# Two matmuls of 128 columns in place of a wide and a narrow one, in some tiles of a transposed product

## The chip, the cores and the metric

The kernel runs on one core of one Trainium2 chip. The metric is the device time of one execution in microseconds (us), as the median of several executions.

## What is computed

One layer of a decoder trunk on 256 tokens of width 2048, all in float32: an input projection, a Mamba-2 scan (SSD) beside sparse attention with a top-64 token indexer, one output projection, and an MLP with a squared ReLU four times as wide.

```python
def hybrid_layer(x, ...):
    h = rmsnorm(x, g_mix) @ w_in                  # 2048 -> 5728
    z, xbc, dt, q, k, v, qi, ki, wi = _split(h, IN_SIZES)
    xbc = jax.nn.silu(causal_dwconv(xbc, conv_w, conv_b))
    ...
    y_ssd = ...                                   # chunked scan, gated, normalised
    y_att = dsa_attention(q, k, v, qi, ki, wi)
    x = x + jnp.concatenate([y_ssd, y_att], axis=-1) @ w_out
    u = rmsnorm(x, g_mlp) @ w_up                  # 2048 -> 8192
    return x + jnp.square(jax.nn.relu(u)) @ w_down
```

## The kernel before

Every large product is made from split operands. `operands` (L113) loads a slab of weights (`raw`), casts it on ScalarE to the rounded float32r form `hi` (L125) and lets VectorE compute the rest `lo = raw - hi` (L126); the activations are kept as `hi` and `lo` too (`hx` for the input projection, `x2x` for the MLP). A product then needs three float32r matmuls for each pair of tiles: hi by hi, lo by hi and hi by lo.

There are two kinds of product. `product` (L138) puts tokens on partitions: the activations are the stationary operand, up to 512 weight columns move (lines L148 to L150). `product_t` (L184) puts columns on partitions: a 128x128 tile of weights is stationary, and the 256 tokens move. The row `right(kt)` holds, side by side, 256 columns of activations `hi` and 256 of `lo`. It runs over 4 slabs of 8 tiles, 32 tiles in all, into two accumulators of 512 columns in PSUM. The left half of an accumulator (columns 0 to T = 256) gathers hi by hi, the right half the two corrections; `total` (L207) adds the halves afterwards. `product_t` serves the index queries (`qi`, 4 products), the convolution's channels (`xbc`, 6 products) and the whole up-projection (`w_up`, 32 products). All its matmuls stand at L201.

TensorE's order is written by hand: the program order is the engine's order. Small matmuls of the scan, the indexer and the attention (transposes, scores, statistics) are tasks that `step()` lets in between tiles, at L204 after every fourth tile of `product_t`. Each takes a PSUM bank through `mp` (L131), which appends to the list `entry`; a finished `product` appends to it as well (L181). So `entry` is not empty exactly when other matmuls have run on TensorE since the last tile of a `product_t`.

Such a tile has a form of its own (L195 to L197). The ordinary tile is three matmuls of 256 columns: weights `hi` by x `hi`, weights `lo` by x `hi`, weights `hi` by x `lo`. Behind other matmuls it is two: weights `hi` by all 512 columns in one, then weights `lo` by x `hi`. Each matmul brings a load of its stationary tile of its own; the profile lists them under PEld.

In the MLP the order is: up-projection quarters 0 and 1 in one go, down-projection quarter 0, up 2, down 1, up 3, down 2, down 3 (L818 to L822). The first of the up-projection's products still has residual tasks between its tiles (`split_rows`, transposes at L672); after that nothing comes between the tiles until a `product` of the down-projection.

Of the kernel before, what the change touches and what calls it, by code (L numbers as in the profile page):

```python
# [16 lines left out]
P = 128  # L17
D = 2048
T = 256
# [49 lines left out]
def hymba_kernel(ctx: ExitStack, tc: tile.TileContext, xn, xt, w_in, w_out, w_up, w_down, vcol, vrow, out):  # L69
# [28 lines left out]
    def step():  # L98
        for t in list(tasks):
            if isinstance(t[1], int) and t[1] > 0:  # L100
                t[1] -= 1
            elif not isinstance(t[1], str) or t[1] in done:
                advance(t)
# [9 lines left out]
    def operands(src, n, load=None, shift=0):  # L113

        with tc.high_priority(offset=HP):
            raw = wts.tile([P, n], F32, name="raw", tag="raw", bufs=RB)
            both = wts.tile([P, 2 * n + SPARE], F32R, name="w2", tag="w2", bufs=WB)
            hi, lo = both[:, shift:shift + n], both[:, shift + n:shift + 2 * n]
            step = n if load is None else n // 2
            for i in range(0, n, step):  # L120
                s = slice(i, i + step)
                nc.sync.dma_start(raw[:, s], src[:, s])
                if load is not None:
                    load()
                nc.scalar.copy(hi[:, s], raw[:, s])  # L125
                nc.vector.tensor_tensor(lo[:, s], raw[:, s], hi[:, s].bitcast(F32), op=OP.subtract)  # L126
        return hi, lo

    entry = []

    def mp(name):  # L131
        entry.append(name)
        return ps.tile([P, 512], F32, name=name, tag="mid")

    def accumulators():
        return [ps.tile([P, 512], F32, name="acc", tag="acc") for _ in range(2)]

    def product(src, n, left, load=None, tail=None):  # L138


        acc = accumulators()
        last = KT if tail is None else KT - 4

        def part(kt, out, b, wh, wl):
            s = slice(b * P, (b + 1) * P)
            ah, al = left(kt)
            free = tail is not None
            nc.tensor.matmul(out, ah[:, s], wh, start=(kt == 0), stop=False, skip_group_check=free)  # L148
            nc.tensor.matmul(out, al[:, s], wh, start=False, stop=False, skip_group_check=free)  # L149
            nc.tensor.matmul(out, ah[:, s], wl, start=False, stop=(kt == KT - 1), skip_group_check=free)  # L150

        kept = []
        halves = [slice(0, n // 2), slice(n // 2, n)]
        if tail is not None:
            acc.append(mp("acc_t"))
        for kt in range(KT):
            if kt % 2 == 0:
                hi, lo = operands(src[kt // 2], 2 * n, load, 0 if tail is None else SPARE - SHIFT_T)
            w = slice(kt % 2 * n, kt % 2 * n + n)
            wh, wl = hi[:, w], lo[:, w]  # L160
            if tail is None:
                for b in range(NB):
                    part(kt, acc[b][:, :n], b, wh, wl)
            elif kt < last:
                for c in halves if kt else [slice(0, n)]:
                    part(kt, acc[0][:, c], 0, wh[:, c], wl[:, c])
                for i, c in enumerate(halves):
                    part(kt, acc[1 + i][:, c], 1, wh[:, c], wl[:, c])
            else:
                kept.append((kt, wh, wl))  # L170
            step()
        if tail is not None:
            for kt, wh, wl in kept:
                for c in halves:
                    part(kt, acc[0][:, c], 0, wh[:, c], wl[:, c])
            tail(0, slice(0, n), acc[0])
            for i, c in enumerate(halves):
                for kt, wh, wl in kept:
                    part(kt, acc[1 + i][:, c], 1, wh[:, c], wl[:, c])
                tail(1, c, acc[1 + i][:, c])  # L180
        entry.append("product")  # L181
        return acc

    def product_t(src, right):  # L184

        acc = accumulators()
        for i in range(4):
            hi, lo = operands(src[i], 1024, shift=SHIFT_T)
            c = i % 2
            for k in range(8):  # L190
                kt = 8 * (i // 2) + k
                x = right(kt)
                s = slice(k * P, (k + 1) * P)

                if entry:  # L195
                    entry.clear()
                    todo = [(hi, 0, 0, 2 * T), (lo, T, 0, T)]  # L197
                else:
                    todo = [(hi, 0, 0, T), (lo, T, 0, T), (hi, T, T, T)]
                for j, (w, at, fr, n) in enumerate(todo):  # L200
                    nc.tensor.matmul(acc[c][:, at:at + n], w[:, s], x[:, fr:fr + n], start=(kt + j == 0),  # L201
                                     stop=(kt == KT - 1 and j == len(todo) - 1), skip_group_check=True)
                if k % 4 == 3:
                    step()  # L204
        return acc
# [58 lines left out]
    def in_block(name, load=None):  # L264
        o, n = in_off[name]
        src = w_in[o:o + n * D].rearrange("(g p c) -> g p c", g=8, p=P)
        return product(src, n, h_left, load)

    def in_pair(name, i):
        o = in_off[name][0] + i * 256 * D  # L270
        return product_t(w_in[o:o + 256 * D].rearrange("(h p c) -> h p c", h=4, p=P), lambda kt: hx[:, kt, :])
# [39 lines left out]
    def stats():  # L311
        nc.sync.dma_start(vr, vrow)
        sst1 = small.tile([P, NB], F32, name="sst1", tag="sst1")
        nc.vector.tensor_reduce(out=sst1, in_=ss1, axis=AX.X, op=OP.add)
        rsqrt(rstd, sst1, 1.0 / D, "x", nc.vector)
        done.add("rstd")

        dg = mid.tile([P, NB, P], F32, name="dg", **u2)
        for b in range(NB):
            nc.vector.tensor_scalar(dg[:, b, :], ident, rstd[:, b:b + 1], None, op0=OP.mult)  # L320
        yield Y["rr"]
        pt = mp("ps_r")
        for b in range(NB):
            nc.tensor.matmul(pt[:, b * P:(b + 1) * P], ones, dg[:, b, :], start=True, stop=True)
        nc.scalar.copy(rrow, pt[:, :T])
# [9 lines left out]
    def transposes(src, n, name):  # L335
        pt = mp(f"pt_{name}")
        for i in range(n):
            nc.tensor.transpose(pt[:, i * P:(i + 1) * P], src[:, i * P:(i + 1) * P], ident)
        return pt
# [368 lines left out]
    def run():  # L708
# [58 lines left out]
        for j in range(4):  # L767
            spawn(residual(j, product(w_out[j], 512, y_left)), f"res{j}")
# [4 lines left out]
    def x2(kt):  # L773
        if kt >= KT - 4:
            need("res3")
        return box[0][:, kt, :]

    first = product_t(w_up[0], x2)
    while tasks:
        step()  # L780
# [11 lines left out]
    def up(q):  # L792
        uh = mlp.tile([P, KT, T], F32R, name="uh")
        ul = mlp.tile([P, KT, T], F32R, name="ul")
        for j in range(8):
            r = mlp.tile([P, 2, T], F32, name="r")
            total(r, first if q + j == 0 else product_t(w_up[8 * q + j], x2))
            nc.vector.scalar_tensor_tensor(r, r, 0.0, r, op0=OP.max, op1=OP.mult)
            s = slice(2 * j, 2 * j + 2)
            nc.scalar.copy(uh[:, s, :], r)  # L800
            nc.vector.tensor_tensor(ul[:, s, :], r, uh[:, s, :].bitcast(F32), op=OP.subtract)
        return uh, ul

    def down(q, u):
        for j in range(4):

            def add(b, c, acc):
                c = slice(512 * j + c.start, 512 * j + c.stop)
                nc.vector.scalar_tensor_tensor(xr[:, b, c], acc, rs4[:, b:b + 1], xr[:, b, c], op0=OP.mult, op1=OP.add)  # L809
                if q == 3:  # L810
                    nc.sync.dma_start(out[b * P:(b + 1) * P, c], xr[:, b, c])

            end = q == 3 and j == 3
            acc = product(w_down[4 * q + j], 512, lambda kt: (u[0][:, kt, :], u[1][:, kt, :]), tail=add if end else None)
            for b in range(0 if end else NB):
                add(b, slice(0, 512), acc[b])
# [58 lines left out]
```

## Time and profile before

| | us |
|---|---|
| median of 3 runs | 1104.3 (1104.14 to 1104.31) |
| the profiled execution's own time | 1106.19 |
| its span, first to last instruction | 1104.1 |
| TensorE busy with matmuls (PE), share of the span | 1093.8, 99% |
| TensorE weight loads (PEld) | 993.5, 90% |
| VectorE (DVE) | 691.8, 63% |
| ScalarE (ACT) | 534.3, 48% |
| 16 DMA engines, busy share of the main queue | 58.2% |

A matmul's listed duration runs from its start to the modelled end of its drain, and the next starts long before that, so what a matmul costs is read from start to start, or from the pieces of the chain of waits, which run from end to end: a piece with its time and its count gives the time for one.

### The profile page before, as it was taken

What the parts mean: (1) busy time and instruction counts of PE and PEld (TensorE: products, weight loads), DVE (VectorE), ACT (ScalarE), POOL (GpSimd) and SP (SyncE); (2) the same over time, 40 slices, a digit from 0 to 9 for tenths busy, and PEclk for the clock granted to TensorE, in tenths of its full rate; (3) what the DMA queues carried; (4) which work ended last, traced back from release to release, by engine and by line L of the source; (5) the groups of instructions that cost most, each with busy time, mean ns of one, the idle gap of its engine ahead of it and who ended that gap; (6) DMA issues with size and microseconds to landing.
All of it is one profiled execution on the core that took longest, in us unless ns stands there. A gap on an engine that the chain in (4) does not pass through costs nothing.

```text
span 1104.1 us, 17665 instructions
## 1 busy us (share of the span) xinstructions
PE 1093.8 (99%) x7052; PEld 993.5 (90%) x7052; DVE 691.8 (63%) x976; ACT 534.3 (48%) x749; POOL 42.5 (4%) x41
## 2 busy tenths in 40 slices
PE   9999998999999999999999999999999999999998
PEld 7999997888888899999998889998889999888888
DVE  6796989677765565666655545665555665555443
ACT  7755554555765544444444334444334454333331
POOL 0020131122000000000000000000000000000000
PEclk9999999999999999999999999999999999999999
DMA  9856444643375555555556655566665566666662
GB/s 296 277 204 189 147 119 151 213 155 120 128 248 189 175 189 186 184 187 191 189 182 194 199 191 191 191 194 193 197 196 193 192 192 193 196 195 197 209 210 77
DMA packets 63745, 207.53 MB, mean 188 GB/s; under 512 B 7216, under 2 KB 11568, under 8 KB 63664
## 3 DMA queue, kind: packets, MB, share of 16 engines
q1 hardware_dynamic: 63520, 206.36, 58.2%
q8 instruction: 55, 0.90, 0.3%
q14 instruction: 26, 0.21, 0.1%
q10 hardware_dynamic: 144, 0.05, 0.0%
HBM read 204.29 MB, written 2.10 MB: 187 GB/s over the span
## 4 chain that ended last, share of the span: by engine, by line
PE 92%; DVE 3%; DMA 3%; ACT 1%; issue 1%; SPq 0%; ACTq 0%; DVEq 0%
PE acc L201 40%; PE acc L150 16%; PE acc L148 16%; PE acc L149 16%; DMA raw<-in_w_in 2%; DVE bc L517 1%; DVE w L126 1%; PE ps_y L588 1%; DMA xrow<-in_xn 1%; DVE sc L481 1%; PE ps_sr L672 0%; PE ps_l L626 0%; PE ps_o L651 0%; ACT w L125 0%; PE ps_dec L579 0%
## 5 line engine op out<-in xcount | busy, mean ns | idle before, releaser
L126 DVE TENSOR_TENSOR w<-raw,w 128x1024 fp32r<-128x1024 f32 (+3 forms) x400 | 466.9, 1170 | 379.5 <-ACT w L125 378.8
L125 ACT CAST w<-raw 128x1024 fp32r<-128x1024 f32 (+3 forms) x400 | 399.5, 1002 | 492.6 <-PE acc L150 255.5
L201 PE MATMUL acc<-x2x,w 128*128 128x256 f32 (+1 forms) x3067 | 355.9, 279 | 0.0
L201 PEld LDWEIGHTS acc<-x2x,w 128*128 128x128 f32 x3067 | 355.3, 188 | 0.5
L148 PE MATMUL acc<-w,uh 128*128 128x512 f32 (+1 forms) x527 | 199.9, 379 | 0.0
L149 PE MATMUL acc<-w,ul 128*128 128x512 f32 (+1 forms) x527 | 199.8, 379 | 0.0
L150 PE MATMUL acc<-w,uh 128*128 128x512 f32 (+1 forms) x527 | 199.8, 379 | 0.0
L150 PEld LDWEIGHTS acc<-w,uh 128*128 128x128 f32 x527 | 98.9, 188 | 18.8
L148 PEld LDWEIGHTS acc<-w,uh 128*128 128x128 f32 x527 | 98.9, 188 | 18.7
L149 PEld LDWEIGHTS acc<-w,ul 128*128 128x128 f32 x527 | 98.9, 188 | 18.7
L201 PE MATMUL acc<-hx,w 128*128 128x256 f32 (+1 forms) x942 | 114.7, 281 | 0.0
L201 PEld LDWEIGHTS acc<-hx,w 128*128 128x128 f32 x942 | 111.4, 188 | 0.9
L148 PE MATMUL acc<-w,hx 128*128 128x512 f32 (+1 forms) x224 | 85.5, 382 | 1.1 <-ACT w L125 1.1
L150 PE MATMUL acc<-w,hx 128*128 128x512 f32 (+1 forms) x224 | 83.2, 372 | 2.8 <-DVE w L126 2.6
L149 PE MATMUL acc<-w,hx 128*128 128x512 f32 (+1 forms) x224 | 82.6, 369 | 0.2 <-DVE hx L241 0.2
L150 PEld LDWEIGHTS acc<-w,hx 128*128 128x128 f32 x224 | 42.7, 191 | 11.0 <-DVE w L126 4.4
L148 PEld LDWEIGHTS acc<-w,hx 128*128 128x128 f32 x224 | 42.7, 191 | 8.4 <-ACT w L125 1.9
L149 PEld LDWEIGHTS acc<-w,hx 128*128 128x128 f32 x224 | 42.7, 191 | 6.9 <-issue 0.7
L809 DVE SCALAR_TENSOR_TENSOR xr<-acc,rs,xr 128x512 f32<-128x512 f32 (+1 forms) x32 | 22.3, 736 | 9.2 <-PE acc L150 9.2
L211 DVE TENSOR_TENSOR r<-acc,r 128x256 f32<-128x256 f32 x64 | 26.8, 418 | 0.0
L148 PE MATMUL acc<-w,yah 128*128 128x512 f32 x64 | 25.7, 402 | 0.0
L148 PE MATMUL acc<-w,ysh 128*128 128x512 f32 x64 | 25.1, 392 | 0.0
(220 smaller groups left out, 730.1 us busy)
## 6 DMA issues: line engine op xcount, KB each, us to landing
raw<-in_w_up SPq DMA_DIRECT2D x128, 512.0 KB, 3.4
raw<-in_w_down SPq DMA_DIRECT2D x128, 512.0 KB, 3.4
raw<-in_w_in SPq DMA_DIRECT2D x72, 512.0 KB, 3.6
raw<-in_w_out SPq DMA_DIRECT2D x32, 512.0 KB, 3.4
raw<-in_w_in SPq DMA_DIRECT2D x16, 256.0 KB, 4.7
raw<-in_w_in SPq DMA_DIRECT2D x16, 152.0 KB, 5.1
raw<-in_w_in SPq DMA_DIRECT2D x8, 304.0 KB, 2.8
xT<-in_xt SPq DMA_DIRECT2D x16, 128.0 KB, 4.6
```

The source lines that it names most:

```text
L125: nc.scalar.copy(hi[:, s], raw[:, s])
L126: nc.vector.tensor_tensor(lo[:, s], raw[:, s], hi[:, s].bitcast(F32), op=OP.subtract)
L148: nc.tensor.matmul(out, ah[:, s], wh, start=(kt == 0), stop=False, skip_group_check=free)
L149: nc.tensor.matmul(out, al[:, s], wh, start=False, stop=False, skip_group_check=free)
L150: nc.tensor.matmul(out, ah[:, s], wl, start=False, stop=(kt == KT - 1), skip_group_check=free)
L201: nc.tensor.matmul(acc[c][:, at:at + n], w[:, s], x[:, fr:fr + n], start=(kt + j == 0), stop=(kt == KT - 1 and j == len(todo) - 1), skip_g ...
L211: nc.vector.tensor_tensor(dst[:, c, :], acc[c][:, :T], dst[:, c, :], op=OP.add)
L481: nc.vector.scalar_tensor_tensor(sc[:, :nk], rl[:, i, :nk], wis[:, b, h:h + 1], neg[:, T - nk:] if first else sc[:, :nk], op0=OP.mult, op1 ...
L517: nc.vector.scalar_tensor_tensor(o[:, j, :], pad[:, j, k:k + T], vcp("conv_w", 12 * k + ct), o[:, j, :], op0=OP.mult, op1=OP.add)
L588: nc.tensor.matmul(pt[:, 64 * i:64 * i + 64], m[i // 4][:, i % 4, :], xdt[:, c, 64 * h:64 * h + 64], start=True, stop=True)
L809: nc.vector.scalar_tensor_tensor(xr[:, b, c], acc, rs4[:, b:b + 1], xr[:, b, c], op0=OP.mult, op1=OP.add)
```

## The change

A tile of `product_t` always starts from the three matmuls of 256 columns. Where other matmuls have run since the last tile (the list is now called `other`), the first of the three, weights `hi` by x `hi`, is issued as two matmuls of 128 columns into the two halves of the same 256 columns of the accumulator. So the tile behind other matmuls has four matmuls of 128, 128, 256 and 256 columns where it had two of 512 and 256. The columns streamed in all are the same, 768. No DMA, no operation of another engine and no buffer changes.

```diff
-                if entry:
-                    entry.clear()
-                    todo = [(hi, 0, 0, 2 * T), (lo, T, 0, T)]
-                else:
-                    todo = [(hi, 0, 0, T), (lo, T, 0, T), (hi, T, T, T)]
+                todo = [(hi, 0, 0, T), (lo, T, 0, T), (hi, T, T, T)]
+
+                if other:
+                    other.clear()
+                    todo[:1] = [(hi, 0, 0, P), (hi, P, P, T - P)]
                 for j, (w, at, fr, n) in enumerate(todo):
                     nc.tensor.matmul(acc[c][:, at:at + n], w[:, s], x[:, fr:fr + n], start=(kt + j == 0),
                                      stop=(kt == KT - 1 and j == len(todo) - 1), skip_group_check=True)
```

## Rows read from the trace of the kernel before

**Rows 1.** The page: busy time by engine; the chain's shares by line.
```profile
PE 1093.8 (99%) x7052; PEld 993.5 (90%) x7052; DVE 691.8 (63%) x976; ACT 534.3 (48%) x749; POOL 42.5 (4%) x41
PE acc L201 40%; PE acc L150 16%; PE acc L148 16%; PE acc L149 16%; DMA raw<-in_w_in 2%; DVE bc L517 1%; DVE w L126 1%; PE ps_y L588 1%; DMA xrow<-in_xn 1%; DVE sc L481 1%; PE ps_sr L672 0%; PE ps_l L626 0%; PE ps_o L651 0%; ACT w L125 0%; PE ps_dec L579 0%
```

**Rows 2.** Groups by shape: L201's matmuls; count | busy us, mean ns | idle.
```profile
L201 PE MATMUL acc<-x2x,w 128*128 128x256 f32 x3062 | 354.6, 278 | 0.0
...
L201 PE MATMUL acc<-hx,w 128*128 128x256 f32 x924 | 109.7, 278 | 0.0
...
L201 PE MATMUL acc<-hx,w 128*128 128x512 f32 x18 | 7.9, 440 | 0.0
...
L201 PE MATMUL acc<-x2x,w 128*128 128x512 f32 x5 | 2.2, 431 | 0.0
```

**Rows 3.** Chain of waits, up-projection: start us, us, what, xcount of matmuls.
```profile
401.59 176.67 PE acc L201 x1499
...
665.33 87.06 PE acc L201 x767
...
839.45 86.60 PE acc L201 x763
```

**Rows 4.** Stretches: us, busy us (count) PE, PEld, DVE, ACT, POOL; clock; DMA.
```profile
401.30:578.00 176.70, 176.70 (x1502) 176.65 (x1501) 108.70 (x134) 82.52 (x111) 0.00 (x0) 1.00 0.58 186
...
665.10:752.20 87.10, 87.10 (x769) 87.02 (x768) 54.30 (x63) 41.34 (x54) 0.00 (x0) 1.00 0.61 194
```

**Rows 5.** L201's weight loads in those two stretches: ns min/median/max.
```profile
L201 PEld LDWEIGHTS acc<-x2x,w x1499: 187/188/192, 401.3 to 577.9; 128*128 128x128 f32 x188
...
L201 PEld LDWEIGHTS acc<-x2x,w x767: 187/188/188, 664.9 to 752.0; 128*128 128x128 f32 x192
```

**Rows 6.** Chain of waits from 55 to 150 us, index queries and convolution.
```profile
55.80 7.07 PE acc L201 x59
62.86 0.24 PE ps_cs L458 x2
...
68.90 0.44 PE ps_r L324 x4
69.34 6.83 PE acc L201 x59
...
78.44 21.79 PE acc L201 x191
...
101.18 4.24 PE acc L201 x35
...
120.04 11.32 PE acc L201 x95
...
131.79 10.91 PE acc L201 x95
```

**Rows 7.** Timeline of TensorE at two wide matmuls: start us, us, instruction.
```profile
101.02 0.40 PE L201 MATMUL acc<-hx,w 128*128 128x512 f32 x1
...
101.25 0.40 PE L201 MATMUL acc<-hx,w 128*128 128x256 f32 x2
...
665.16 0.40 PE L201 MATMUL acc<-x2x,w 128*128 128x512 f32 x1
...
665.40 0.40 PE L201 MATMUL acc<-x2x,w 128*128 128x256 f32 x2
```

**Rows 8.** Chain of waits, float32 matmuls of 256, then of 128 columns.
```profile
239.37 1.73 PE ps_l L626 x8
...
249.24 0.89 PE ps_l L626 x8
```

**Rows 9.** Waits of TensorE by releaser: us in total, times, longest us.
```profile
PE ps_cb L551 <- ACT bc L519: 0.9, 1, 0.9
PE ps_ki L398 <- DVE kd L393: 0.6, 1, 0.6
```

**Rows 10.** Chain of waits between 150 and 170 us.
```profile
150.68 0.67 PE acc L201 x5
...
165.66 2.06 DVE bc L517
```

More of the change, by code (lines that the diff above doesn't have):

```diff
@@ L127, in operands @@
         return hi, lo
-    entry = []
+    other = []
     def mp(name):
-        entry.append(name)
+        other.append(name)
         return ps.tile([P, 512], F32, name=name, tag="mid")
@@ L180, in product @@
                 tail(1, c, acc[1 + i][:, c])
-        entry.append("product")
+        other.append("product")
         return acc
```

## The prediction

> **What bounds the kernel now.** I read the busy times and the chain's shares first: TensorE is busy for 99% of the span, and of the chain that ends last L201 alone is 40%, the other products' three lines 48% [rows 1]. So time on TensorE is time of the kernel, except where a wait swallows it. Next the groups by shape: L201 has 18 + 5 = 23 wide matmuls of 512 columns [rows 2], one for each tile behind other matmuls. These 23 tiles of 42 x 32 = 1344 are all that the change rewrites; a price of some tenths of a microsecond for each would move the total by a few microseconds.
>
> The chain in order of time shows what makes these few tiles matter. The stretch from 401.59 has 1499 matmuls in 176.67 us, 117.9 ns each; the one from 665.33 has 767 in 87.06, 113.5 ns each, and the one from 839.45 763 in 86.60, 113.5 [rows 3]. The program is the same in all three: the same line, operands and shape. The granted clock is 1.00 in both stretches (the 2.4 GHz level), the DMA share 0.58 and 0.61 [rows 4], TensorE is never idle. The weight loads differ slightly: up to 192 ns in the slower stretch, 188 at most in the faster one [rows 5]. The earlier products show it too, between equal counts: 59 matmuls take 7.07 us at 55.80 and 6.83 at 69.34; 95 take 11.32 at 120.04 and 10.91 at 131.79 [rows 6]. With the first, wide one taken out (0.236, below), these are 117.8 and 113.7 ns, 117.9 and 113.6; the long stretches give (176.67 - 0.24)/1498 = 117.8 and (87.06 - 0.24)/766 = 113.3. So TensorE has two rhythms for the same work, 4.4 ns apart, and whichever a stretch has, it keeps on average to its end, 1499 matmuls in one case. A stretch begins each time with a tile behind other matmuls: with just the tile that is rewritten.
>
> **The change part by part: the 23 tiles.** Now such a tile takes the wide matmul, 101.02 to 101.25 or 665.16 to 665.40, 0.236 us (the rows' 0.23 and 0.24, rounded starts) [rows 7], and a narrow one of about 0.118: 0.354 us. After, it has two of 128 columns and two of 256. The two of 256 cost 0.1133 to 0.1178 each, 0.231 together. For a float32r matmul of 128 columns there is no row. Bounds: by columns alone it is half of 0.1133, 0.057 us, and the tile 0.114 + 0.227 = 0.341, that is 0.013 less than now. At the far end it streams like plain float32, where 128 columns come as two passes of 0.89/8 = 0.111 [rows 8], 0.222 in all; the tile is then 0.444 + 0.231 = 0.675, 0.321 more. Between them stands the load: each matmul brings its own load of a 128x128 tile, and small matmuls don't get under it: 16 columns take 0.24/2 = 0.12 us, 128 columns 0.44/4 = 0.11 [rows 6], while 256 columns of float32, 1.73/8 = 0.216, are set by the streaming [rows 8]. I take 0.111, the load's pace, as the nearest row by size of load and columns. The tile is 0.222 + 0.231 = 0.453 us, 0.099 more than now.
>
> The Trainium skill ("TensorE: Matmul & The Clock Gate", section "Back-to-back issue gap") gives about 81 ns per matmul for a stream of load and matmul pairs of 128 columns. By that figure the tile would be an estimated 0.393 us, 0.04 more than now, and the whole change 1.1 us cheaper than I sum it; no matmul of 128 columns or fewer is below 0.11 in the rows [rows 6, 8].
>
> **What of it lies on the path.** The first of the 23 (at 43.5 us) is followed by a wait of 0.6 us for VectorE (L393), which takes it up; and from 150.68 to 165.66 the chain leaves TensorE for VectorE's convolution and scores, and TensorE waits 0.9 us at L551 [rows 9, 10]. Three tiles start in there, and 3 x 0.1 fits into 0.9. If these covers were gone, they would cost 0.4 us. So 23 - 4 = 19 tiles count: 19 x 0.099 = 1.9 us, with bounds of 19 x -0.013 = -0.2 and 19 x 0.321 = 6.1. ScalarE and VectorE have nothing to do with the tile but make the slabs, and they are ahead: TensorE loses no time to them in the long stretches [rows 4]. If L201 gets faster there, slabs are wanted as often as from 665.10 on, where DMA ran at 194 GB/s without a stall [rows 4]. No wait is added, no queue is passed; 46 matmuls and 46 loads are.
>
> **The change part by part: the rhythm.** Slow now, and on the path: the 1499, 11 just ahead of them (between the transposes of L672), and from 55 to 150 us stretches of 59, four of 35, 23 and 95, 317 together [rows 3, 6]. Turned to the fast rhythm they give 1510 x 4.44 ns = 6.7 us and 317 x 4.44 = 1.4 us: 8.1. Fast now: the two long stretches, 2 x 767 x 4.44 = 6.8 us to lose, and seven shorter ones, of which those of 59, 191 and 95 are shown, 437 in all, 1.9 us [rows 3, 6].
>
> What a stretch starts behind decides, as far as rows tell. Behind the index scores, float32r of 256 columns at 0.12 us apart (the one at 101.18 stands for eight), all are slow; behind transposes some are fast and some slow, as the two of 95 show; behind L324, four matmuls at the load's pace, the stretch at 69.34 is fast [rows 6]; behind the 512-column matmuls of a product (665.33, 839.45) it is fast [rows 3]. After the change every stretch starts alike: two matmuls at the load's pace come between the others and the first of 256 columns. The nearest row to that is the one behind L324, and it is fast. I therefore take the fast rhythm for all, knowing that it rests on one likeness: a wide matmul stood in between there, too.
>
> Sum for the forecast: the profiled execution's span is 1104.1, its own time 1106.19, with 2.1 us around the span that the change doesn't touch; 1104.1 + 1.9 - 8.1 = 1097.9 span. The median without the profiler, 1104.3, lies 1.9 below the profiled time: too little for the 1499 to run fast in it (6.7). So the difference of -6.2 carries over: 1098.1 us.
>
> **The rivals.** (1) The rhythm stays where it is in each stretch, because something further back decides it, such as where in SBUF the two reads, of moving columns and of the next weights, stand when the stretch starts. Then only the price is left: 1104.3 + 1.9 = 1106.2. For it speaks that stretches behind transposes came out both ways with the same tile ahead of them. The Trainium skill, same page and section, has one gap for a matmul of 256 columns (262 cycles, an estimated 109 ns) and no second rhythm; by it alone nothing but the price could come of the change. The trace shows two, 113.3 and 117.8.
> (2) Slower, by one mechanism: the load's pace ahead of the first 256 columns sets the slow rhythm, as behind most transposes, which run at 0.11 too. The point from which it decides is whether the stretches at 665 and 839, which now start behind a streaming matmul of 512 columns, are caught: 1106.2 + 6.8 = 1113.0, and with the 437 1114.9. For it speaks that these two lose the start that made them fast.
> (3) A swap: the 1499 turn fast, the two long ones slow: 1106.2 - 6.7 + 6.8 = 1106.3.
> (4) 128 columns of float32r stream at float32's price: 6.1 in place of 1.9, so 1110.4 with rhythms as now, 1102.3 with all fast. Against it: every other float32r matmul, 256 columns and up, costs one pass.
> That the change does not do what it says can't be: the lines issue four matmuls.
>
> **How the numbers follow.** All fast 0.43 (1098.1; 1099.5 if the early 317 stay slow, 1095.8 at the lower bound of the price); as now 0.22 (1104.1 to 1106.6); swap or one long stretch of the two turned 0.10 (1103 to 1110); both long ones slow 0.17 (1113 to 1115); float32's price 0.08 (1102 to 1110). The range from 1096 to 1110.5 leaves out case 2 and little else. About 0.2%, 2.2 us, can be told from no change: below 1102.1 counts as faster, 0.44; up to 1106.5 as the same, mostly rival 1 and part of the swap, 0.22; above that 0.34. Faster and slower both being likely, the forecast's own range is 1096 to 1101.
>
> **What would show it.** In the changed profile: no L201 matmul of 512 columns, 46 of 128, 7098 matmuls in all; the starts of the 128s 0.11 apart (0.22 for rival 4); the piece of 1499, now 1501 matmuls, at 170 us (fast) or 177; the two of 767, now 769, at 87 or 90.6; ps_cb's and ps_ki's waits shorter by a tenth or three. Wrong it would be if the long pieces keep or change their rhythm against this, or if the two 128s cost less than one load.

## The result and the profile after

| | before | after |
|---|---|---|
| median, us | 1104.3 (1104.12 to 1105.49, 5 runs) | 1098.82 (1098.5 to 1099.35, 5 runs) |
| ratio | | 0.995, 95% interval 0.9935 to 0.9964 |
| span of the profiled execution, us | 1104.1 | 1096.5 |

The change makes the kernel faster by 5.5 us, between 4.0 and 7.2 by the interval. The forecast was 1098.1.

From the page after, busy time by engine. Beside [rows 1] it has 46 more matmuls and 7.4 us less of TensorE's busy time:

```profile
PE 1086.4 (99%) x7098; PEld 987.4 (90%) x7098; DVE 689.8 (63%) x976; ACT 534.5 (49%) x749; POOL 42.0 (4%) x41
```

The groups by shape after, as in [rows 2], with the transposed product's matmuls at L200 now: the 23 wide ones are gone, 46 of 128 columns have come.

```profile
L200 PE MATMUL acc<-x2x,w 128*128 128x256 f32 x3067 | 348.8, 276 | 0.0
...
L200 PE MATMUL acc<-hx,w 128*128 128x256 f32 x942 | 111.1, 278 | 0.0
...
L200 PE MATMUL acc<-hx,w 128*128 128x128 f32 x36 | 6.8, 270 | 0.0
...
L200 PE MATMUL acc<-x2x,w 128*128 128x128 f32 x10 | 1.8, 266 | 0.0
```

The chain of waits after, as in [rows 3] (start us, us, what, count), in the up-projection:

```profile
395.01 2.86 PE acc L200 x25
...
400.23 170.12 PE acc L200 x1501
...
657.42 87.18 PE acc L200 x769
...
831.66 87.18 PE acc L200 x769
```

and between 50 and 150 us, as in [rows 6]:

```profile
54.50 6.96 PE acc L200 x61
...
67.92 6.93 PE acc L200 x61
...
100.07 4.22 PE acc L200 x37
...
118.88 11.02 PE acc L200 x97
...
130.34 11.02 PE acc L200 x97
```

The stretch of 1499 matmuls in 176.67 us is one of 1501 in 170.12: 113.3 ns each. Equal counts now take equal times: 6.96 and 6.93, 11.02 twice. From start to start the trace has 113.3 ns in every one of the 23 stretches once they have settled. The long stretch's weight loads have 192 ns at the most still, but that is the first tile's; the median is 188 as in the fast stretch of [rows 5], and the matmuls' median duration has gone from 281 to 276 ns, which marks the fast rhythm in what follows:

```profile
L200 PEld LDWEIGHTS acc<-x2x,w x1501: 187/188/192, 400.0 to 570.0; 128*128 128x128 f32 x188
L200 PE MATMUL acc<-x2x,w x1500: 274/276/334, 400.0 to 570.0; 128*128 128x256 f32 x187, 128*128 128x128 f32 x1
```

Where the span's 7.6 us went, by the chain's starts in the two traces: 1.3 us lie ahead of 55.80 (54.50 after), where only the first rewritten tile stands; that one begins 1.4 us earlier in the trace after, before anything was changed, and in the kernels below it begins anywhere from 41.4 to 42.6 us (43.5 in the trace of before), so I put this down to scatter in the start-up. From there to 150.68 nothing (94.88 and 94.91 us). From 150.68 to the up-projection -0.3. Its first half, 396.57 to 665.33 before and 395.01 to 657.42 after, -6.35: the gain. The rest pays 0.3. So the change itself is worth 6.3 us in this pair of traces, and 5.5 by the medians. The start of that half in the trace of before:

```profile
396.57 2.74 PE acc L201 x23
```

### The profile page after: what moved, and what is told of

Same layout as the page of the kernel before. It is cut to its first block, busy times and chain, and to the rows that moved or that the text cites. A ratio compares the mean times of both kernels' runs of the same rounds, so it can differ in the third digit from the quotient of the medians.

```text
span 1096.5 us, 17759 instructions
## 1 busy us (share of the span) xinstructions
PE 1086.4 (99%) x7098; PEld 987.4 (90%) x7098; DVE 689.8 (63%) x976; ACT 534.5 (49%) x749; POOL 42.0 (4%) x41
## 4 chain that ended last, share of the span: by engine, by line
PE 92%; DVE 3%; DMA 2%; issue 1%; ACT 1%; SPq 0%; ACTq 0%; DVEq 0%
PE acc L200 40%; PE acc L148 16%; PE acc L150 16%; PE acc L149 16%; DMA raw<-in_w_in 2%; DVE w L126 1%; DVE bc L516 1%; PE ps_y L587 1%; DMA xrow<-in_xn 1%; PE ps_sr L671 0%; PE ps_l L625 0%; PE ps_o L650 0%; ACT w L125 0%; PE ps_dec L578 0%; DVE sc L480 0%
## 5 line engine op out<-in xcount | busy, mean ns | idle before, releaser
L200 PE MATMUL acc<-x2x,w 128*128 128x256 f32 (+1 forms) x3077 | 349.8, 276 | 0.0
L200 PEld LDWEIGHTS acc<-x2x,w 128*128 128x128 f32 x3077 | 349.4, 188 | 0.2
L200 PE MATMUL acc<-hx,w 128*128 128x256 f32 (+1 forms) x978 | 114.9, 277 | 0.0
L200 PEld LDWEIGHTS acc<-hx,w 128*128 128x128 f32 x978 | 112.7, 188 | 0.0
```

## The experiments

All have the same operands and DMA transfers and differ from one of the two kernels in the shapes of a few matmuls of the transposed product alone. The rhythm of a stretch is read from start to start in the settled part, or from the matmuls' median duration (276 ns fast, 281 slow).

### Neither form: ordinary tiles behind other matmuls

```diff
-                if other:
-                    other.clear()
-                    todo[:1] = [(hi, 0, 0, P), (hi, P, P, T - P)]
```

> Every tile of the transposed product is the ordinary three matmuls of 256 columns, also behind other matmuls. Theory (the pair at the load's pace sets the fast rhythm): without the pair stretches behind index scores (117 to 120 ns apart) stay slow at 117.8 ns, those behind transposes go either way; with the 1499 slow the time is about 1104 to 1106 us. Rival A (the wide matmul of 512 columns is what makes a stretch slow, and anything without it is fast): all stretches run at 113.3 ns, the tile is 0.340 us against 0.453 in the changed kernel, so 19 x 0.11 = 2.1 us under the changed kernel, about 1096.7 us.

Measured: 1105.88 us (1104.70 to 1106.82, 10 runs), ratio 1.0012 (1.0003 to 1.0021) to the kernel before. Its chain of waits:

```profile
99.63 4.24 PE acc L197 x36
...
118.50 10.90 PE acc L197 x96
...
399.98 170.02 PE acc L197 x1500
...
657.06 90.45 PE acc L197 x768
...
834.58 90.45 PE acc L197 x768
```

The total is where the theory put it, but for another reason. The stretch of 1500 is fast (170.02/1500 = 113.3 ns), and the two long ones behind a product, fast before, are slow (90.45/768 = 117.8). It is the swap of the third rival, 6.7 us won and 6.8 lost. Rival A falls: without a wide matmul stretches are slow too, behind the index scores all of them, and behind the 512-column matmuls of a product just as well. So what stood at the start of those two stretches mattered, and the ordinary tile loses it.

Two other stretches of this run bear on the likeness that the prediction rested on. They start right behind float32 matmuls at the load's pace, 0.11 us apart, with no wide matmul in between: the first behind four of 16 columns, the second behind the four that stand at L324 in the kernel before (L320 here):

```profile
61.15 0.22 PE ps_cs L455 x2
61.37 5.75 PE acc L197 x48
67.12 0.45 PE ps_r L320 x4
67.57 7.08 PE acc L197 x60
```

Both are slow (117.8 ns from start to start once settled). In the kernel before, with a wide tile behind the same matmuls, both were fast at 113.3 (6.83 us for 59 behind L324 [rows 6]). So matmuls at the load's pace just ahead of the first 256 columns do not by themselves make a stretch fast.

### The split form in one tile alone

```diff
+                    entries.append(i)
                     todo = [(hi, 0, 0, 2 * T), (lo, T, 0, T)]
+                    if len(entries) == 21:
+                        todo = [(hi, 0, 0, P), (hi, P, P, T - P), (lo, T, 0, T), (hi, T, T, T)]
```

> The kernel before, with the split form in one tile alone: the last one behind transposes in the first up-projection product (at 401.35 us), from which the stretch of 1499 starts. Theory: that stretch turns from 117.8 to 113.3 ns and nothing else changes: 1499 x 4.44 ns = 6.7 less, 0.1 more for the tile, so 1104.3 - 6.6 = 1097.7 us, about 1 us under the changed kernel, which pays the price in all 23 tiles. Rival B (the rhythm depends on what happened further back, and the change shifted all of it): the stretch stays at 117.8 and the time at 1104.3.

Measured: 1098.87 us (1098.37 to 1099.20, 4 runs), ratio 0.9949 (0.9932 to 0.9966). Its chain:

```profile
100.55 4.24 PE acc L205 x35
...
401.16 170.13 PE acc L205 x1501
...
658.36 87.06 PE acc L205 x767
```

One tile brings the whole gain: the 1501 run at 113.3 ns, the stretches behind the index scores stay slow. Rival B falls. The 1 us under the changed kernel that was expected did not come: the time is that of the changed kernel (1098.82) within the scatter. So the other 22 split tiles neither win nor lose anything that can be measured: what the early stretches gain goes into the price of the tiles.

### A split tile, and a wide one, in the middle of the long stretch

The first adds to the kernel before, the second to the changed one, one tile where no other matmul is near:

```diff
+                if mark and kt == 8 and i == 2:
+                    todo = [(hi, 0, 0, P), (hi, P, P, T - P), (lo, T, 0, T), (hi, T, T, T)]
```

```diff
+                if mark and kt == 8 and i == 2:
+                    todo = [(hi, 0, 0, 2 * T), (lo, T, 0, T)]
```

> The kernel before, with one more tile in the split form in the middle of the slow stretch of 1499, where no other matmul is near (product 8 of the up-projection, third slab, first tile: 260 tiles after the stretch's start). Theory (the pair resets the rhythm wherever it stands): about 780 matmuls at 117.8 ns, then about 720 at 113.3, so 720 x 4.44 = 3.2 us less: 1101.2 us. Rival B (only what TensorE did before the stretch, or a switch from another kind of matmul, sets it): 117.8 to the end of the stretch, 1104.4 us.

> The changed kernel, with the wide and narrow form in one tile in the middle of the fast stretch of 1501 (product 8 of the up-projection, third slab, first tile). Theory (the wide matmul does not set a rhythm, it only hands on the one it finds): 113.3 ns before and after it, 0.01 us more. Rival A (the wide matmul throws the stretch into the slow rhythm): about 720 matmuls at 117.8 ns after it, 3.2 us more than the changed kernel, about 1102.0 us.

Measured: 1100.75 and 1101.58 us. L203's matmuls in the first, ahead of and behind the marked tile (ns min/median/max, first and last start):

```profile
L203 PE MATMUL acc<-x2x,w x707: 281/281/281, 401.7 to 484.9; 128*128 128x256 f32 x177
...
L203 PE MATMUL acc<-x2x,w x690: 276/276/276, 491.8 to 569.9; 128*128 128x256 f32 x173
```

L202's in the second:

```profile
L202 PE MATMUL acc<-x2x,w x735: 276/276/276, 401.8 to 485.0; 128*128 128x256 f32 x184
...
L202 PE MATMUL acc<-x2x,w x665: 281/281/281, 491.8 to 570.0; 128*128 128x256 f32 x167
```

The split tile turns a slow stretch fast, with no switch from other matmuls near. The wide tile turns a fast stretch slow, which the theory had not expected: a wide matmul does not merely hand on the rhythm that it finds. Yet in the kernel before the stretches that began with a wide tile behind a product were fast, so the wide form has no fixed outcome.

### The forms, and the places

One run has seven wide tiles in the long stretch of the changed kernel and between them other cuts of the same columns; another has seven wide tiles at seven different places in their products, each followed by a split tile. The forms, as widths of the matmuls in order ("hi" and "lo" name the weights):

```python
"wide":    hi 512, lo 256
"split":   hi 128, hi 128, lo 256, hi 256
"128+384": hi 128, hi 384, lo 256
"384+128": hi 384, hi 128, lo 256
"64+192":  hi 64, hi 192, lo 256, hi 256
"third":   hi 256, lo 256, hi 128, hi 128
```

> The changed kernel, with one marked tile (third slab, first tile) in each of products 1 to 13 of the up-projection, inside the long stretch. The wide form, which made a fast stretch slow in the run before, stands in products 1, 3, 5, 7, 9, 11 and 12; between them other forms of the first tile are tried from the slow rhythm: 384 + 128 columns of hi then lo (product 2), 128 + 384 then lo (4), 64 + 192 then lo and hi (6), the third matmul halved in place of the first (8), the split form (10, 13). Theory (a matmul at the load's pace anywhere in the tile resets the rhythm): every one of 2, 4, 6, 8, 10, 13 turns 117.8 to 113.3 ns. Rival C (it has to be the matmul just ahead of the next one of 256 columns, so that this one starts when its weights come in and not when the array is free): 384 + 128, 64 + 192, the halved third and the split turn it, 128 + 384 does not, since 384 columns outlast the load. Rival D (it has to be the split of the first matmul as it is): only 10 and 13. Product 12, wide from the slow rhythm: stays slow. About 7 segments of 96 matmuls slow at 4.44 ns each, some 3 us over the changed kernel, up to 6 if the forms fail.

> The changed kernel, with a wide tile in products 1, 3, 5, 7, 9, 11, 13 of the up-projection at seven different places (slab 0 tile 2, 0/5, 1/1, 1/4, 2/3, 3/0, 3/6), and a split tile in products 2, 4, ... 14 at the third slab's start. Theory (the sequence of widths decides, not the addresses): all seven wide tiles turn 113.3 to 117.8 ns, all seven split tiles turn it back. Rival E (the buffer and address of the tile decide): some of each do not turn. About 7 x 100 matmuls slow, 3 us over the changed kernel, 1102 us, and 0.8 for seven more split tiles.

Measured: 1102.62 and 1103.07 us. L214's matmuls in the run with the forms, behind the 384 + 128 tile, the 128 + 384 tile, the wide tile that came next, and the halved third matmul:

```profile
L214 PE MATMUL acc<-x2x,w x73: 276/276/276, 425.8 to 433.9; 128*128 128x256 f32 x73
...
L214 PE MATMUL acc<-x2x,w x79: 281/281/281, 447.2 to 456.4; 128*128 128x256 f32 x79
...
L214 PE MATMUL acc<-x2x,w x78: 276/276/276, 458.8 to 467.5; 128*128 128x256 f32 x78
...
L214 PE MATMUL acc<-x2x,w x73: 276/276/276, 492.3 to 500.5; 128*128 128x256 f32 x73
```

From the slow rhythm 384 + 128, the halved third and the split (twice) turn the stretch fast; 128 + 384 does not. That is rival C's pattern: the narrow matmul has to come last, just ahead of the next one of 256 columns. The 64 + 192 tile was not tested here, since the wide tile ahead of it, coming from a slow stretch, had turned fast. Where a wide tile came from a fast stretch, five of five in this run turned it slow; of the two that came from a slow one, one turned it fast (product 5) and one left it slow (product 12).

In the run with the places all seven wide tiles turned the stretch from 113.3 to 117.8 ns, and all seven split tiles turned it back. The wide tiles stood at seven different places, the split ones at the third slab's start in seven products: no tile failed to turn the stretch, so rival E falls here. L212's matmuls behind the first of each:

```profile
L212 PE MATMUL acc<-x2x,w x104: 281/281/281, 410.8 to 422.9; 128*128 128x256 f32 x104
...
L212 PE MATMUL acc<-x2x,w x46: 276/276/276, 425.3 to 430.4; 128*128 128x256 f32 x46
```

The same run has one stretch that stayed slow behind a split tile, though not in the long stretch: the 61 matmuls from 54.36 us on, behind the transposes of the index keys. L212's matmuls in it:

```profile
L212 PE MATMUL acc<-hx,w x37: 281/281/281, 55.7 to 60.0; 128*128 128x256 f32 x37
```

Its first four starts agree within 3 ns with those of the same tile in the changed kernel's first trace, where the stretch is fast. So the split form comes close to certain and is not.

### The price of a split tile

```diff
-                if other:
+                if other or more and k % 4 == 0:
```

`more` is set for all but the first product of the up-projection.

> The changed kernel, with the split form also in two more tiles of each slab (first and fifth) of 31 products of the up-projection: 248 tiles, of which 2 follow a product anyway: 246 more. The rhythm is fast there already, so this is the price alone. Forecast's price against an ordinary tile in the fast rhythm: 0.453 - 0.340 = 0.113 us, so 27.8 us more than the changed kernel, about 1126.6 us. By columns alone: nothing. By float32's price for 128 columns: 246 x 0.335 = 82 us more.

Measured: 1130.56 us. Its chain:

```profile
401.13 185.33 PE acc L200 x1621
...
673.51 95.16 PE acc L200 x832
```

Against the changed kernel's 170.12 for 1501 and 87.18 for 769, that is 15.21 us for 120 more split tiles and 7.98 for 63: 0.127 us for each, where 0.113 was expected. The starts of one such tile (from 407.89 us) tell why. From the first 128 to the second they are 57 ns apart, from there to lo 113, from lo to the last hi 170: 340 for three loads, 113 each and not 111; and the next four gaps are 117, 119, 116 and 114 before the rhythm settles, 13 ns over 4 x 113.3. One more load at 113 and 13 of settling make 0.127: a float32r matmul of 128 columns adds a load and not float32's price, so rival 4 of the prediction is out.

### How narrow, and how many

```python
"448+64": hi 448, hi 64, lo 256          # and in the same way 320+192, 304+208, 272+240, 256+256
"448+32+32": hi 448, hi 32, hi 32, lo 256   # and 320+96+96
"192+64": hi 192, hi 64, lo 256, hi 256     # and 64+192
```

> The changed kernel, with wide tiles in products 1, 3, 5, 7, 9, 11 of the up-projection to make the stretch slow, and behind each a tile whose 512 columns of hi are cut at another place, then lo: 384 + 128 (product 2), 320 + 192 (4), 448 + 64 (6), 304 + 208 (8), 272 + 240 (10), 256 + 256 (12). Theory (the matmul just ahead of the next one of 256 has to be shorter than a load, so that the next starts with its weights): at 0.443 ns a column and a load of 0.11 to 0.114 us, 64, 128, 192 and 208 columns (0.03 to 0.09 us) turn the stretch to 113.3 ns; 240 (0.106) is at the edge; 256 (0.113) doesn't. Rival F (only 128 columns, the half of a tile, does): 384 + 128 alone turns it. Time: six segments of 96 slow at 4.44 ns, 2.6 us over the changed kernel.

Measured: 1104.32 us. L217's matmuls behind the 320 + 192 and the 448 + 64 tile:

```profile
L217 PE MATMUL acc<-x2x,w x79: 281/281/281, 447.8 to 456.9; 128*128 128x256 f32 x79
...
L217 PE MATMUL acc<-x2x,w x79: 281/281/281, 470.3 to 479.4; 128*128 128x256 f32 x79
```

Here the theory in this form fell, and rival F did not: from the slow rhythm 384 + 128 alone turned the stretch fast, as it had before. 320 + 192 and 304 + 208 left it slow, though their last matmul is shorter than a load, and 448 + 64, coming from a fast stretch, made it slow. 272 + 240 came from a fast one too and left it fast. 256 + 256 changed nothing, from slow to slow. What the forms that had never failed have in common is two short matmuls: the split's two of 128, the two halves of the third. That made a new theory, one matmul at the load's pace is not enough to be sure, two in a row are, and the next run tests it, with a split and a wide tile ahead of each form so that each starts from a slow stretch:

> The changed kernel, in products 1 to 14 of the up-projection seven times in turn: a split tile (to make the stretch fast), then a wide one (to make it slow), then a tile with another cut of hi: 64 + 192 and 192 + 64 (then lo and hi of 256), 448 + 32 + 32 and 320 + 96 + 96 (then lo), 448 + 64, 320 + 192 and 384 + 128 (then lo). Refined theory (two matmuls in a row that are shorter than a load set the fast rhythm, whatever their widths; with one it depends on the widths and on what was before): the first four turn 117.8 to 113.3 ns; of the last three 384 + 128 does and 320 + 192 doesn't, as seen, and 448 + 64 is not told. Rival (only widths of 128 do it): of all seven only 384 + 128 turns the stretch.

Measured: 1103.47 us. L220's matmuls behind 64 + 192, 192 + 64, 448 + 32 + 32, 320 + 96 + 96, and behind 320 + 192:

```profile
L220 PE MATMUL acc<-x2x,w x64: 276/276/276, 424.3 to 431.5; 128*128 128x256 f32 x64
...
L220 PE MATMUL acc<-x2x,w x64: 276/276/276, 446.8 to 453.9; 128*128 128x256 f32 x64
...
L220 PE MATMUL acc<-x2x,w x64: 276/276/276, 469.3 to 476.4; 128*128 128x256 f32 x64
...
L220 PE MATMUL acc<-x2x,w x64: 276/276/276, 491.8 to 498.9; 128*128 128x256 f32 x64
...
L220 PE MATMUL acc<-x2x,w x66: 281/281/281, 535.8 to 543.5; 128*128 128x256 f32 x66
```

All four forms with two short matmuls in a row turn the slow stretch fast, at four widths from 32 to 192, so it is not the width of 128. Of the forms with one, 320 + 192 fails again, 384 + 128 succeeds again, and 448 + 64 turns the stretch fast, this time from a slow one.

### A cheaper tile, and the changed kernel again

```diff
-                    todo[:1] = [(hi, 0, 0, P), (hi, P, P, T - P)]
+                    todo = [(hi, 0, 0, 3 * P), (hi, 3 * P, 3 * P, P), (lo, T, 0, T)]
```

> In every tile behind other matmuls the 512 columns of hi are issued as 384 and 128, then lo with 256: three matmuls in place of the changed kernel's four. Theory: this tile resets the rhythm too, so all stretches run at 113.3 ns, and it takes 0.403 us where the split tile and its settling take 0.453 to 0.477: 19 x 0.05 to 0.074 = 1.0 to 1.4 us under the changed kernel, about 1097.6 us. Rival G (what turned a slow stretch doesn't settle one that comes from other matmuls): some of the 23 stretches are slow, up to the time of the kernel before, 1104 us, if the 1499 are among them.

> The changed kernel once more, unaltered, beside the 384 + 128 form on the same chip: 1098.8 us, every stretch at 113.3 ns.

Measured side by side: 1098.67 us (1097.88 to 1099.44, 5 runs), ratio 0.9944 (0.9930 to 0.9957), and for the changed kernel 1099.43 (1097.93 to 1100.59, 5 runs), 0.9952 (0.9939 to 0.9964). The two can't be told apart, so the 1.0 to 1.4 us that were expected did not come. The chain of the cheaper tile:

```profile
118.43 11.37 PE acc L200 x96
...
130.23 10.97 PE acc L200 x96
...
400.55 170.07 PE acc L200 x1500
```

Five of its 23 stretches are slow, all behind transposes, the one at 118.43 among them; the long one is fast. That is rival G, without the 1500: behind other matmuls a form with one short matmul goes either way.

## Why the prediction was right

**The rhythm.** The step that carried the forecast, that all stretches would take the fast rhythm, holds: 23 of 23 in the trace after, 23 of 23 in the changed kernel's second trace. The row that it was read from does not bear it out, and to that extent the forecast was lucky. It rested on one likeness, the stretch behind L324 [rows 6], four matmuls at the load's pace. The prediction called it thin, since a wide matmul stood in between there. With ordinary tiles nothing stands in between, and the stretch behind the same four matmuls is slow, as is the one behind four of 16 columns. And the wide matmul does not just hand on what it finds: put into a fast stretch it made it slow, 23 of 23 tiles counted over five kernels.

What the runs bear out is narrower: two float32r matmuls in a row inside the tile, each shorter by its columns than a load, set the fast rhythm. In the middle of a slow stretch the split form did so 11 times of 11, and five other tiles with such a pair (the halved third matmul, 64 + 192, 192 + 64, 448 + 32 + 32, 320 + 96 + 96) once each. Behind other matmuls, in the eight kernels with the split form in all 23 places, it did so 183 times in 184; the miss is the stretch shown above. The 16-column matmuls, which did not help the ordinary tile, are float32 and stand ahead of the tile; which of the two makes the difference no run separates. With no such pair in the tile the outcome depends on what came before.

**The sizes.** Forecast for the 1499: -6.7 and three tiles' price of 0.1 each; the chain has -6.35 from 396.57 on, against -6.4. The early stretches were to win 1.4 us, less the price of 13 tiles, 1.3; the chain has +0.03. From 150.68 to the up-projection a price of 0.1 was forecast and -0.3 came, and for the two tiles from 665.33 on 0.2, where the rest pays 0.3. Together that is -6.3 in this pair of traces where -6.2 was forecast. The tile's price was put 0.014 too low: 0.127 us over an ordinary tile in place of 0.113, for the load's pace is 113 and not 111 ns here and the settling was left out. Over 19 tiles that is 0.27 us. The sign "the starts of the 128s 0.11 apart" did not come: their loads are 0.11 apart, the two starts 57 ns inside a stretch and 143 behind the transposes ahead of the long one. By its own terms the lowest time that the prediction names, 1095.8, is 1104.3 - 8.1 - 0.2 = 1096.0.

**The covers.** The waits that were to hide four tiles are there and shorter, as foreseen, 0.5 us each in place of 0.6 and 0.9 [rows 9]:

```profile
PE ps_ki L397 <- DVE kd L392: 0.5, 1, 0.5
PE ps_cb L550 <- ACT bc L518: 0.5, 1, 0.5
```

**The supply.** With the fast rhythm the long stretch wants its slabs faster, and gets them at the rate that [rows 4] showed for 665.10 on; the stretch's row after:

```profile
400.00:570.00 170.00, 170.00 (x1503) 170.00 (x1501) 108.54 (x131) 82.70 (x111) 0.00 (x0) 1.00 0.61 193
```

**The rivals.** That the rhythm would stay where it is (1106.2) is refuted by the one split tile. The slower case did not come, and its mechanism, the load's pace in the tile setting the slow rhythm, is refuted by the split tiles. What spoke for it is real: the two long stretches can lose the start that made them fast, and with ordinary tiles they do, 90.45 us in place of 87.06. The swap that was given as the third rival is what the ordinary tiles make, by a form that the prediction did not consider.

**What stays open.** What inside TensorE holds a rhythm for 1499 matmuls is not shown. The traces give its marks alone: in the slow rhythm a third of the weight loads take 192 ns in place of 188, and the starts repeat with the three matmuls of a tile, 353.3 ns a tile against 340.

These marks show that the slow rhythm comes in two kinds. The 192 ns load is that of each tile's first matmul in every slow stretch that begins with a wide tile, and that of its second (lo) in those that 128 + 384, 320 + 192 or 304 + 208 left slow. With three states in place of two the outcomes in the middle of a stretch fall into order: no form that was tried more than once from the same state gave two results. The wide tile turns fast to the first kind (23 of 23), keeps the first kind (2 of 2) and turns the second kind fast (3 of 3); 384 + 128 turns the first kind fast (3 of 3), 320 + 192 turns it to the second (2 of 2). This was found in the finished traces; no run was made to test it. Nor is it shown why one short matmul works at 128 columns behind 384 and not at 192 behind 320.

## What to carry to other kernels

When the same matmul with the same operands has two durations in two stretches of one trace, compare stretches of equal count in the chain, and look at what each begins with: here one tile's shape was worth 6.5 us over the next 1499 matmuls, twenty times the upper bound that the prediction put on the tile's own cost. A tile that sets a rhythm pays only where a long stretch follows: at 0.11 us more than the wide tile and 4.4 ns a matmul, from about 26 matmuls on, which fits that one split tile did as well as 23. Test such a tile from both states, in the middle of a stretch, and at more than one width: from one state alone several forms looked like a cure that were not.

## What the runs showed of the hardware that was not expected

In these runs TensorE, at a granted clock of 1.00, ran a stream of load and matmul pairs of 256 float32r columns in one of two stable rhythms, 113.3 or 117.8 ns a pair, and changed between them only where the shapes change. A single matmul of 512 columns in a fast stream made it slow each time (23 of 23), for as long as the stream lasted, some 700 matmuls in one case; two float32r matmuls in a row of 32 to 192 columns made a slow one fast (16 of 16). The Trainium skill ("TensorE: Matmul & The Clock Gate", section "Back-to-back issue gap") has about 81 ns a pair at 128 columns. No run here has a long stream of such pairs; inside the tiles the starts took 340 ns for three loads, at two matmuls of 128 columns (57, 113 and 170) as at two of 32 (26, 112 and 202), so the load, at 113 ns, set the pace.
